# Scale and shift of x's blocks, and the gate unit's normalisation, written by ScalarE instead of VectorE in a hybrid HGRN2/gMLP block

## The chip, the cores and the metric

The kernel runs on one core of a Trainium2 chip. Its time is the device time of one execution in microseconds (us). PE is the matmul engine, PEld its weight loads, DVE the vector engine, ACT the scalar engine, POOL GpSimd, SP the engine that issues the DMAs.

## The reference

One layer of a diffusion backbone on x (2048 positions, 1024 channels) with a context of 256 positions, in fp32. Cut to what matters here:

```python
def modulate(h, shift, scale):
    return h * (1.0 + scale) + shift
...
h = modulate(rmsnorm(x, norm_mix[l]), sh1, sc1)
o, _, _ = token_mixers(h @ w_in[l], lb_f, lb_b, first, hf_c, hb_c, *mix_args)
x = x + g1 * (o @ w_out[l])
h2 = modulate(rmsnorm(x, norm_ffn[l]), sh2, sc2)
x = x + g2 * conv_ffn(h2, w_up[l], conv_w[l], conv_b[l], w_down[l], rows)
```

`token_mixers` has a gated linear recurrence (4 heads) and a gate unit (4 heads, chunks of 128 positions) on the same projection:

```python
def chunk_sgu(u, v, ln_g, ln_b, w_s, b_s):
    ...
    u = jax.nn.gelu(u, approximate=False).reshape(bsz, n, MLP_CHUNK, MLP_HEADS, MLP_DIM)
    v = jax.nn.gelu(v, approximate=False).reshape(bsz, n, MLP_CHUNK, MLP_HEADS, MLP_DIM)
    v = layernorm(v, ln_g.reshape(MLP_HEADS, MLP_DIM), ln_b.reshape(MLP_HEADS, MLP_DIM))
    z = jnp.einsum('hpq,bnqhc->bnphc', w_s.astype(v.dtype), v) + jnp.transpose(b_s)[None, None, :, :, None]
    return (u * z).reshape(bsz, t, MLP_WIDTH)
```

The change touches `modulate` of the first `h` and the inner part of `layernorm`, (v - mean) times the reciprocal deviation.

## The kernel before

**Precision.** Every large product of fp32 operands is made of three products of two halves. `split` (L131, L132) writes the high half of a tile by a cast on ACT and the low half by a subtraction on DVE or POOL; `mm3` or the loop in `run_banks` adds high x high, high x low and low x high into one PSUM bank. All matmuls are recorded at L65 and all transpositions at L69, so tile names tell them apart.

**Stages.** Until about 50 us the modulation vectors are made and the context is normalised, transposed and split (`ctx_mod`, L313). Then `run_banks` goes through a hand-written order of product banks until about 980 us: per bank eight blocks of weights (`whi`, `wlo`, split from `raw` by `split_w`, two slots that alternate) times the rows of x (`xh`, `xl`), three products for each of the eight blocks, 128x512 results in a bank with the tag `pj`, which a sink then reads. After that come the output projection and the gated MLP, up to the end.

The first banks are those of the context ("c", 256 columns wide), then "g" and "v" on x's first half, in the order `c c c c c c g c g c v c q c q c s c s s c s t c t t t`. Side work is put between the products by two queues: `Pump.slot` runs what is due, by a clock of modelled PE time (`T.t`); a generator says with `yield 1.6` how long it wants to wait. In this way:

- `x_start` and `x_first` (16 blocks of 128x512, some 55 to 95 us): rows are squared and summed on ACT (`xjk`, L231), the reciprocal deviation `rs` comes from POOL (L124, L126), DVE scales the rows `xk` (L237), PE transposes four 128x128 blocks into a bank of the tag `mi`, and `x_mod` (L239 to L244) scales and shifts the bank with the columns `a1` and `s1` into the tile `xfl` and splits it into `xh` and `xl`. For odd blocks DVE writes `xl`, for even blocks POOL.
- `x_second` (32 blocks of 128x256, some 112 to 200 us) does the same for x's second half, through `sp` into DRAM (`xh_d`, `xl_d`), from which it is loaded again later.
- the sinks: `silu` (a sigmoid `sig` on ACT and a product on DVE), `sink_gate` and `sink_gate_x` (sigmoids on ACT: `cf`, `cS`, later F and K), and `sgu` for the gate unit.

`xfl` and `sig` share one tag with two buffers. The tag `mi` has three banks, `pj` three, `sc` two.

**The gate unit.** `sv` evicts a bank with a Gelu on ACT. 4.6 us of modelled time later `ln` transposes it into an `mi` bank, takes mean and variance on DVE (`bn_stats`, `bn_aggr` into `mv`), the reciprocal deviation on POOL (`rstd`, L124 and L126), and writes `nt` in four pieces of 128x128 (L699). 7.0 us later `mix` multiplies `nt` by the position matrix (`wsT`). There are 16 such normalisations, from 141 to 976 us.

**Order.** Outside `manual_schedule` and apart from pinned instructions, a scheduler orders each engine's instructions by priorities and its own cost model. A changed engine or price thus also changes the order of neighbouring instructions.

Of the kernel before, what the change touches and what calls it, by code (L numbers as in the profile page):

```python
# [9 lines left out]
F32 = mybir.dt.float32  # L10
# [3 lines left out]
AF = mybir.ActivationFunctionType  # L14
ALU = mybir.AluOpType
# [3 lines left out]
P = 128  # L19
# [29 lines left out]
def view(t, off, dims):  # L49

    return bass.AP(t.tensor, t.offset + off, [list(t.ap[0])] + [list(d) for d in dims])
# [32 lines left out]
def tile_trunk(ctx, tc, x, c, cx, c_ctx, w_ada, b_ada, norm_mix, norm_ffn, w_in, hg_norm, sgu_g, sgu_b,  # L84
               w_sp, b_sp, w_out, w_up, conv_w, conv_b, w_down, norm_final, masks, out):
    nc = tc.nc
    V, S, G, T = nc.vector, nc.scalar, nc.gpsimd, Tensor(nc.tensor)
# [19 lines left out]
    a1 = cst.tile([P, 2, 8], F32, name="a1")  # L107
    s1 = cst.tile([P, 2, 8], F32, name="s1")
# [12 lines left out]
    def rstd(pool, ss, n, scale, bias=EPS, keep=lambda i: i, out=None):  # L121

        r = pool.tile([P, 8], F32, tag="rs", name="rs")
        keep(G.tensor_scalar(out=r[:, :n], in0=ss, scalar1=scale, scalar2=bias, op0=ALU.mult, op1=ALU.add))  # L124
        r2 = pool.tile([P, 8], F32, tag="rs2", name="rs2") if out is None else out
        G.tensor_tensor(out=r2[:, :n], in0=r[:, :n], in1=mhalf[:, :n], op=ALU.pow)  # L126
        return r2

    def split(hi, lo, raw, eng=None, keep=lambda i: i):

        keep(S.copy(hi, raw))  # L131
        (eng or G).tensor_sub(lo, raw, hi.bitcast(F32))  # L132
# [56 lines left out]
    with es1:  # L189
        ps = es1.enter_context(tc.tile_pool(name="ps1", bufs=1, space=PSUM, reuse_waits="tile"))  # L190
        p1 = es1.enter_context(tc.tile_pool(name="p1", bufs=1, reuse_waits="tile"))
        pm = es1.enter_context(tc.tile_pool(name="pm", bufs=1, reuse_waits="tile"))
# [10 lines left out]
        def bank(tag):  # L203
            return ps.tile([P, 512], F32, tag=tag, name=tag, bufs={"pj": 3, "sc": 2, "mi": 3}[tag])
# [34 lines left out]
        def x_mod(pt, which, k, hi, lo, n, eng):  # L239

            fl = pm.tile([P, 512], F32, tag="sig", name="xfl", bufs=2)
            V.tensor_scalar(out=fl[:, :n], in0=pt, scalar1=a1[:, which, k:k + 1], scalar2=s1[:, which, k:k + 1],
                            op0=ALU.mult, op1=ALU.add)
            split(hi, lo, fl[:, :n], eng)  # L244

        def rows_of(src, t0, n):
# [146 lines left out]
        def x_first(g0, xs):  # L393
            for k in range(NK):
                pt = bank("mi")
                for i in range(4):
                    pin(T.transpose(pt[:, i * P:(i + 1) * P], xs[i][:, k * P:(k + 1) * P], ident))
                sl = slice(g0 * P, g0 * P + 512)
                x_mod(pt, 0, k, xh[:, k, sl], xl[:, k, sl], 512, V if k % 2 else G)
                if k % 2:  # L400
                    yield 1.6
# [24 lines left out]
        def x_second():  # L426

            xk = pk.tile([P, 2, D], F32, tag="K", name="xk2", bufs=2, align_bytes=AL)
            sp = pk.tile([P, 4, 512], F32R, tag="K", name="sp", bufs=2, align_bytes=AL)
            xs = [xk[:, 0, :], xk[:, 1, :]]  # L430
            n = 0
            for g in range(0, NCH, 2):
                for i in range(2):
                    ld(xs[i], x_rows[NCH + g + i])
                yield 6.0
                ss = x_sums()
                x_square(xs, ss)
                x_scale(xs, ss)
                yield 6.0
                for k in range(0, NK, 2):  # L440
                    pt = bank("mi")
                    for kk in range(2):
                        for i in range(2):
                            o = kk * 256 + i * P
                            pin(T.transpose(pt[:, o:o + P], xk[:, i, (k + kk) * P:(k + kk + 1) * P], ident))
                    b = 2 * (n % 2)
                    n += 1
                    for kk in range(2):
                        sl = slice(kk * 256, kk * 256 + 256)
                        x_mod(pt[:, sl], 0, k + kk, sp[:, b, sl], sp[:, b + 1, sl], 256, V if kk else G)  # L450
                    for t, d in ((0, xh_d), (1, xl_d)):
                        st(d[:, k:k + 2, g * P:g * P + 256], sp[:, b + t, :].bitcast(F32).rearrange("p (k c) -> p k c", k=2))
                    yield 2.2
# [214 lines left out]
        def sgu(hh, h):  # L668

            z, u = {}, {}  # L670

            def both(n0):
                if n0 in z and n0 in u:
                    zt = z.pop(n0)
                    G.tensor_mul(zt, zt, u.pop(n0))
                    st(oT_d[hh][:, 4 + h, n0:n0 + 512], zt)

            def su(n0, n, pj):
                u[n0] = pm.tile([P, 512], F32, tag="gu", name="gu", bufs=2)
                S.activation(u[n0], pj, AF.Gelu)  # L680
                both(n0)

            def sv(n0, n, pj):
                gv = pm.tile([P, 512], F32, tag="vv", name="gv", bufs=2)
                S.activation(gv, pj, AF.Gelu)

                def ln():
                    pt = bank("mi")
                    for i in range(4):
                        T.transpose(pt[:, i * P:(i + 1) * P], gv[:, i * P:(i + 1) * P], ident)  # L690
                    bs = pm.tile([P, 4, 6], F32, tag="bs", name="bs", bufs=2)
                    mv = pm.tile([P, 4, 2], F32, tag="mv", name="mv", bufs=2)
                    for i in range(4):
                        V.bn_stats(out=bs[:, i, :], in_=pt[:, i * P:(i + 1) * P])
                        V.bn_aggr(out=mv[:, i, :], in_=bs[:, i, :])
                    r = rstd(pm, mv[:, :, 1], 4, 1.0)
                    nt = pm.tile([P, 512], F32, tag="nt", name="nt", bufs=2)
                    for i in range(4):
                        V.tensor_scalar(out=nt[:, i * P:(i + 1) * P], in0=pt[:, i * P:(i + 1) * P],  # L699
                                        scalar1=mv[:, i, 0:1], scalar2=r[:, i:i + 1], op0=ALU.subtract, op1=ALU.mult)  # L700

                    def mix():
                        pz = bank("mi")
                        for i in range(4):
                            T.matmul(pz[:, i * P:(i + 1) * P], nt[:, i * P:(i + 1) * P], wsT[:, h, :],
                                     start=True, stop=True)
                        V.scalar_tensor_tensor(out=nt.rearrange("p (c q) -> p c q", q=P),
                                               in0=pz.rearrange("p (c q) -> p c q", q=P), scalar=sgg[:, h:h + 1],
                                               in1=view(rh, h * P, [[0, 4], [1, P]]), op0=ALU.mult, op1=ALU.add)
                        z[n0] = nt  # L710
                        both(n0)
                    hg_q.later(mix, 7.0)
                hg_q.later(ln, 4.6)
            return su, sv

# [397 lines left out]
        i = len(seq) - 4  # L1113
# [452 lines left out]
    V = Kept(nc.vector, pin)  # L1566
# [243 lines left out]
```

## Time and profile before

| | |
|---|---|
| median of the runs | 2451.37 us (2449.67, 2451.37, 2454.72) |
| profiled execution | 2449.13 us, span 2447.3 us |
| mean granted PE clock | 0.998 |
| PE busy | 2408.3 us, 98% |
| DVE busy | 1785.5 us, 73% |
| ACT busy | 943.7 us, 39% |
| POOL busy | 873.4 us, 36% |
| DMA | 163 GB/s mean |

One execution was profiled. A row of a group gives line, engine, operation, written tile and read tiles, shapes, count, then busy time, mean ns of one, and the idle time of the engine just before, with what ended most of it. A row in the order of time gives start and duration in us, and in brackets the wait before it. "PEclk" is the granted clock of the matmul engine as a share of full speed.

### The profile page before, as it was taken

The numbers are of one execution on the slowest core, as the hardware profiler recorded it, in microseconds if no ns is written. First come the engines' busy times: TensorE is split into PE (matmuls) and PEld (weight loads), VectorE is DVE, ScalarE is ACT, GpSimd is POOL, SyncE is SP. The second block draws the span as 40 slices with busy tenths as digits, with TensorE's granted clock in tenths as the row PEclk, the third lists the DMA queues.
The fourth block names the chain that finished last, engine by engine and source line by source line (L and its number), as shares of the span: only waits on it lengthen the run. The fifth ranks groups of instructions, "written<-read, shape, count | busy, mean of one in ns | idle before, by whom it ended". The sixth has DMA issues, their size and how long they took to land.

```text
span 2447.3 us, 32836 instructions
## 1 busy us (share of the span) xinstructions
PE 2408.3 (98%) x11859; PEld 2000.8 (82%) x11859; DVE 1785.5 (73%) x2445; ACT 943.7 (39%) x1614; POOL 873.4 (36%) x795
## 2 busy tenths in 40 slices
PE   7999999999999999999999999999999999999998
PEld 4788888888888888788788888878888888888887
DVE  5867685756776776466698877769999992776875
ACT  4554334333344433354443333333333342332343
POOL 1232010110111122001688778787778870000002
PEclk9999999999999999999999999999999999999999
DMA  8365446564254234668822222562222238934645
GB/s 310 109 210 171 141 136 209 193 225 147 96 185 155 87 104 149 233 216 261 297 86 88 82 96 83 177 237 85 86 93 94 83 102 349 318 125 146 228 151 197
DMA packets 307855, 400.13 MB, mean 163 GB/s; under 512 B 33113, under 2 KB 216161, under 8 KB 304621
## 3 DMA queue, kind: packets, MB, share of 16 engines
q1 hardware_dynamic: 304404, 397.28, 48.1%
q8 instruction: 94, 1.54, 0.3%
q10 hardware_dynamic: 3289, 0.76, 0.1%
q14 instruction: 68, 0.56, 0.1%
HBM read 288.85 MB, written 109.13 MB: 163 GB/s over the span
## 4 chain that ended last, share of the span: by engine, by line
PE 40%; DVE 7%; issue 3%; POOL 2%; ACT 1%; DMA 0%; SPq 0%; POOLq 0%; ACTq 0%; DVEq 0%
PE up L65 25%; PE dn L65 15%; DVE dn L1377 3%; DVE edges L1382 1%; DVE gp L1458 1%; ACT dn L1374 1%; POOL Al L132 0%; POOL ra L1669 0%; POOL rr L1670 0%; DVE keep L1452 0%; POOL raw L1195 0%; DVE keep L1468 0%; ACT cv L1396 0%; ACT Ah L131 0%; POOL cv L1469 0%
## 5 line engine op out<-in xcount | busy, mean ns | idle before, releaser
L1377 DVE SCALAR_TENSOR_TENSOR dn<-gp,taps,dn 128x1024 f32<-128x1024 f32 x352 | 448.3, 1280 | 21.4 <-ACT dn L1374 18.1
L65 PE MATMUL up<-yf,Ah 128*128 128x512 f32 x1232 | 393.7, 389 | 0.0
L65 PE MATMUL dn<-thl,mhl 128*128 128x512 f32 x1680 | 381.5, 389 | 1.2 <-ACT thl L131 1.2
L132 POOL TENSOR_TENSOR Al<-raw,Ah 128x512 fp32r<-128x512 f32 x264 | 342.9, 1307 | 92.0 <-ACT Ah L131 79.0
L65 PEld LDWEIGHTS dn<-thl,mhl 128*128 128x128 f32 x1680 | 315.0, 188 | 67.7 <-ACT thl L131 2.0
L65 PE MATMUL pj<-xh,whi 128*128 128x512 f32 x896 | 363.1, 406 | 0.0
L65 PE MATMUL pj<-xh,wlo 128*128 128x512 f32 x896 | 350.6, 392 | 2.0 <-DVE wlo L132 2.0
L65 PE MATMUL pj<-xl,whi 128*128 128x512 f32 x896 | 351.4, 392 | 1.1 <-POOL xl L132 1.0
L65 PE MATMUL up<-xah,Al 128*128 128x512 f32 x704 | 275.6, 392 | 3.8 <-POOL Al L132 3.8
L65 PE MATMUL up<-xah,Ah 128*128 128x512 f32 x704 | 274.5, 390 | 0.6 <-ACT Ah L131 0.6
L65 PEld LDWEIGHTS up<-yf,Ah 128*128 128x128 f32 x1232 | 231.2, 188 | 48.1
L131 ACT CAST Ah<-raw 128x512 fp32r<-128x512 f32 x264 | 160.5, 618 | 278.4 <-PE up L65 208.4
L65 PE MATMUL up<-xal,Ah 128*128 128x512 f32 x528 | 205.5, 389 | 0.0
L65 PE MATMUL up<-yf,Al 128*128 128x512 f32 x528 | 205.2, 389 | 0.0
L65 PEld LDWEIGHTS pj<-xh,wlo 128*128 128x128 f32 x896 | 168.3, 188 | 38.2 <-DVE wlo L132 2.7
L65 PEld LDWEIGHTS pj<-xh,whi 128*128 128x128 f32 x896 | 168.6, 188 | 33.3 <-issue 3.5
L65 PEld LDWEIGHTS pj<-xl,whi 128*128 128x128 f32 x896 | 168.8, 188 | 32.2 <-POOL xl L132 1.9
L65 PE MATMUL dn<-wo,o 128*128 128x512 f32 x768 | 182.9, 394 | 2.1 <-ACT o L131 1.6
L580 POOL TENSOR_TENSOR K<-K,tot 128x512 f32<-128x512 f32 x40 | 50.0, 1251 | 343.9 <-PE sc L65 194.5
L65 PEld LDWEIGHTS dn<-wo,o 128*128 128x128 f32 x768 | 141.9, 188 | 31.8 <-ACT o L131 2.0
L65 PEld LDWEIGHTS up<-xah,Al 128*128 128x128 f32 x704 | 132.1, 188 | 36.5 <-POOL Al L132 9.4
L65 PEld LDWEIGHTS up<-xah,Ah 128*128 128x128 f32 x704 | 132.2, 188 | 28.0 <-ACT Ah L131 1.0
(315 smaller groups left out, 3923.7 us busy)
## 6 DMA issues: line engine op xcount, KB each, us to landing
raw<-in_w_up_dram SPq DMA_DIRECT2D x88, 512.0 KB, 4.7
mr<-m SPq DMA_DIRECT2D x85, 512.0 KB, 5.0
raw<-in_w_in_dram SPq DMA_DIRECT2D x68, 512.0 KB, 4.2
sT<-wd SPq DMA_DIRECT2D x88, 256.0 KB, 4.1
raw<-in_w_ada_dram SPq DMA_DIRECT2D x32, 512.0 KB, 3.8
yf<-yd SPq DMA_DIRECT2D x14, 1024.0 KB
m<-cv SPq DMA_DIRECT2D x22, 544.0 KB, 2.7
raw<-in_w_down_dram SPq DMA_DIRECT2D x22, 512.0 KB, 4.3
```

The source lines that it names most:

```text
L65: return self.engine.matmul(out, lhsT, rhs, **kw)
L131: keep(S.copy(hi, raw))
L132: (eng or G).tensor_sub(lo, raw, hi.bitcast(F32))
L580: e.tensor_mul(view(K2, row * W + o, src), view(K, o, src), view(tot, t0, [[4, n], [ts, 2], [0, B]]))
L1374: S.activation(cr, gt[:, 0:RH, 0:GW], AF.Identity, bias=cvb[:, f:f + 1], scale=taps[:, f:f + 1])
L1377: V.scalar_tensor_tensor(out=cr, in0=gt[:, t // 3:t // 3 + RH, t % 3:t % 3 + GW], scalar=taps[:, t * NF + f:t * NF + f + 1], in1=cr, op0=A ...
L1382: V.scalar_tensor_tensor(out=e[:, 0, :], in0=gt[:, 1, t % 3:t % 3 + GW], scalar=taps[:, t * NF + f:t * NF + f + 1], in1=e[:, 0, :], op0=AL ...
L1458: V.tensor_add(g_rows(hh, f + c, n2), quad(p, kind), quad(add, kind))
```

## The change

`x_mod`: the multiplication and addition of a block by two columns is one ACT instruction (Identity with a scale and a bias column) and not one DVE instruction. In the gate unit a tile `nm` of 128x4, minus the mean times the reciprocal deviation, is new on DVE; `nt` is then x times the reciprocal deviation plus `nm`, in four ACT instructions in place of four on DVE.

```diff
         def x_mod(pt, which, k, hi, lo, n, eng):
 
             fl = pm.tile([P, 512], F32, tag="sig", name="xfl", bufs=2)
-            V.tensor_scalar(out=fl[:, :n], in0=pt, scalar1=a1[:, which, k:k + 1], scalar2=s1[:, which, k:k + 1],
-                            op0=ALU.mult, op1=ALU.add)
+            S.activation(fl[:, :n], pt, AF.Identity, bias=s1[:, which, k:k + 1], scale=a1[:, which, k:k + 1])
             split(hi, lo, fl[:, :n], eng)
...
                     r = rstd(pm, mv[:, :, 1], 4, 1.0)
                     nt = pm.tile([P, 512], F32, tag="nt", name="nt", bufs=2)
+                    nm = pm.tile([P, 4], F32, tag="nm", name="nm", bufs=2)
+                    V.scalar_tensor_tensor(out=nm, in0=mv[:, :, 0], scalar=-1.0, in1=r[:, :4], op0=ALU.mult, op1=ALU.mult)
                     for i in range(4):
-                        V.tensor_scalar(out=nt[:, i * P:(i + 1) * P], in0=pt[:, i * P:(i + 1) * P],
-                                        scalar1=mv[:, i, 0:1], scalar2=r[:, i:i + 1], op0=ALU.subtract, op1=ALU.mult)
+                        S.activation(nt[:, i * P:(i + 1) * P], pt[:, i * P:(i + 1) * P], AF.Identity,
+                                     bias=nm[:, i:i + 1], scale=r[:, i:i + 1])
```

## The prediction

> **What bounds the kernel now.** I read the page's busy times first, then the busy times by stretch, then who PE waits for, then the order in time of PE, ACT, DVE and POOL in the one stretch where PE has holes.
>
> ```profile
> span 2447.3 us, 32836 instructions
> PE 2408.3 (98%) x11859; PEld 2000.8 (82%) x11859; DVE 1785.5 (73%) x2445; ACT 943.7 (39%) x1614; POOL 873.4 (36%) x795
> ```
>
> ```profile
> core 0: us, PE busy (x) PEld busy (x) DVE busy (x) ACT busy (x) POOL busy (x), PEclk, DMA share, GB/s
> 50.00:100.00 50.00, 45.12 (x282) 37.84 (x282) 44.69 (x77) 26.49 (x50) 15.21 (x12) 0.97 0.35 109
> 100.00:150.00 50.00, 49.61 (x289) 42.85 (x289) 30.84 (x73) 27.16 (x49) 10.83 (x15) 1.00 0.56 175
> 150.00:200.00 50.00, 49.73 (x273) 42.29 (x272) 37.12 (x84) 24.83 (x45) 21.64 (x23) 1.00 0.62 201
> 200.00:1020.00 820.00, 811.09 (x4599) 697.46 (x4599) 544.25 (x857) 305.99 (x594) 113.04 (x118) 1.00 0.47 158
> 1020.00:2447.00 1427.00, 1413.98 (x6265) 1163.20 (x6263) 1104.52 (x1312) 539.47 (x844) 709.97 (x618) 1.00 0.47 161
> ```
>
> PE, the matmul engine, is busy in 2408.3 of 2447.3 us: it is the bound, and only the 39 us in which it stands idle, or new idle time, can move the end. The stretches say where it stands. The edited lines run from just before the first cast of `xfl` (the row of 56.19 below) to the last `nt`, which starts at 974.8 us by the line's own view:
>
> ```profile
> L699 DVE TENSOR_SCALAR nt<-mi,mv,rs x64: 398/402/410, 141.2 to 974.8; 128x128 f32<-128x128 f32 x64
> ```
>
> In 50 to 100 us PE loses 50.00 - 45.12 = 4.88 us while DVE is busy for 44.69 of 50; from 100 to 200 us it loses 0.66 us, from 200 to 1020 us 8.9 us in 820. So the stretch that matters is 50 to 100 us, where the first half of x is scaled, shifted and split. There the clock granted is 0.97, elsewhere 1.00, so no term below comes from the clock.
>
> **What is removed and added.** These groups carry the prices (busy time, mean ns of one, idle time before them):
>
> ```profile
> L242 DVE TENSOR_SCALAR xfl<-mi,a,s 128x256 f32<-128x256 f32 x32 | 16.1, 532 | 5.3 <-POOL sp L132 3.2 <-PE mi L69 2.0
> L242 DVE TENSOR_SCALAR xfl<-mi,a,s 128x512 f32<-128x512 f32 x16 | 12.7, 802 | 2.5 <-POOL xl L132 2.0 <-PE mi L69 0.4
> L699 DVE TENSOR_SCALAR nt<-mi,mv,rs 128x128 f32<-128x128 f32 x64 | 21.9, 403 | 18.5 <-POOL rs L126 18.5
> ```
>
> ```profile
> L313 ACT ACTIVATE xfl<-mi,s,a 128x256 f32<-128x256 f32 x4 | 2.2, 562 | 5.1 <-DVE s L300 3.9 <-DVE cl L318 1.3
> L549 ACT ACTIVATE cS<-pj 128x256 f32<-128x256 f32 x4 | 1.5, 382 | 0.0
> L977 ACT ACTIVATE sig<-pj 128x512 f32<-128x512 f32 x32 | 19.1, 596 | 38.6 <-PE pj L65 38.1 <-POOL xl L132 0.4
> L622 ACT COPY cdh<-mi 128x128 f32<-128x128 f32 x8 | 2.1, 264 | 7.4 <-DVE hf L623 4.7 <-PE mi L65 2.8
> ```
>
> DVE loses 48 scale-and-shifts and 64 normalisations: 16.1 + 12.7 + 21.9 = 50.7 us. It gains 16 `nm` of 128x4; the nearest row is the 128x4 operation below, 0.16 us, so 2.6 us in all.
>
> ```profile
> 50.27 0.16 DVE L300 TENSOR_TENSOR s<-sc,bc 128x4 f32<-128x4 f32 x1 [0.37 <-PE sc L65]
> ```
>
> ACT gains 112 instructions. The trace has the very form in L313: 128x256 out of PSUM with scale and bias from a column per partition, 562 ns, against 382 ns for L549, the same size without them: 180 ns for the two columns. Added to 596 ns (L977, 128x512) that is 0.78 us, added to 264 ns (L622, 128x128) 0.44 us. ACT gains 16 x 0.78 + 32 x 0.56 + 64 x 0.44 = 59 us. On an engine that is busy for 39% that costs nothing by itself; what counts is the order, because ACT now does both halves of a chain that DVE and ACT shared.
>
> For the same instruction a column operand's price also stands in the Trainium skill, "ScalarE: Activation LUTs", section "What ACT_TABLE_LOAD costs": 186 ns plus 0.833 ns per element plus about 93 ns per column. An estimate by it is 0.80 us for 128x512 and 585 ns for 128x256; L313 measured 562, so it is a little dear here, and the sum below would be 0.1 us longer by it.
>
> **50 to 100 us, step by step.** The rows of PE, ACT, DVE and POOL in the order of time (start, duration, in brackets the wait before):
>
> ```profile
> 64.18 0.39 PE L65 MATMUL pj<-ch,wlo 128*128 128x256 f32 x1 [1.01 <-DVE wlo L132]
> 67.70 0.48 PE L65 MATMUL pj<-xh,whi 128*128 128x512 f32 x1
> 69.43 0.50 PE L65 MATMUL pj<-xh,wlo 128*128 128x512 f32 x1 [0.90 <-DVE wlo L132]
> 75.54 0.30 PE L69 MATMUL mi<-ident,xk 128*128 128x128 f32 x1
> 81.53 0.66 PE L69 MATMUL mi<-ident,xk 128*128 128x128 f32 x4 [0.29 <-DVE xfl L242]
> 82.39 0.66 PE L69 MATMUL mi<-ident,xk 128*128 128x128 f32 x4 [0.20 <-DVE hb L623]
> 87.42 0.66 PE L69 MATMUL mi<-ident,xk 128*128 128x128 f32 x4
> 89.44 0.50 PE L65 MATMUL pj<-xl,whi 128*128 128x512 f32 x1 [0.62 <-POOL xl L132]
> 93.07 0.50 PE L65 MATMUL pj<-xl,whi 128*128 128x512 f32 x1 [0.37 <-POOL xl L132]
> ```
>
> ```profile
> 56.19 1.14 ACT L131 CAST xh<-xfl 128x512 fp32r<-128x512 f32 x2
> 59.46 0.38 ACT L549 ACTIVATE cf<-pj 128x256 f32<-128x256 f32 x1
> 62.33 1.05 ACT L231 ACTIVATE xjk<-xk 128x1024 bf16<-128x1024 f32 x1
> 63.38 0.36 ACT L549 ACTIVATE cf<-pj 128x256 f32<-128x256 f32 x1
> 64.95 1.04 ACT L131 CAST whi<-raw 128x1024 fp32r<-128x1024 f32 x1
> 83.52 0.60 ACT L977 ACTIVATE sig<-pj 128x512 f32<-128x512 f32 x1 [0.44 <-POOL xl L132]
> ```
>
> ```profile
> 67.33 2.05 DVE L132 TENSOR_TENSOR wlo<-raw,whi 128x1024 fp32r<-128x1024 f32 x1
> 74.64 2.74 DVE L237 TENSOR_SCALAR xk<-xk,rs 128x1024 f32<-128x1024 f32 x4
> ```
>
> ```profile
> 67.01 1.29 POOL L132 TENSOR_TENSOR xl<-xfl,xh 128x512 fp32r<-128x512 f32 x1 [4.42 <-ACT xh L131]
> 73.08 0.34 POOL L124 TENSOR_SCALAR rs<-xss 128x4 f32<-128x4 f32 x1
> 73.50 1.11 POOL L126 TENSOR_TENSOR rs<-rs,mhalf 128x4 f32<-128x4 f32 x1
> ```
>
> *What goes.* PE's waits for DVE (1.01 at 64.18, 0.90 at 69.43, 0.29 at 81.53, 0.20 at 82.39) and for POOL's `xl` (0.62 and 0.37) are late products of DVE's queue and of the chain behind `xfl`: 3.39 us. I count all as gone and put in their place what the changed order makes.
>
> *A weight's cast behind two pairs.* In the changed program's order ACT does per pair of blocks `xfl, xfl, xh, xh`, and the cast `whi` of 64.95 stands two pairs later, behind the second pair and one more `xjk`. Two neighbours on ACT overlap by 0.10 us (56.19: two 0.62 casts in 1.14), so from the `cf` at 59.46, which PE releases: two `cf` 0.56, pair 1.36 + 1.04, `xjk` 1.05 (62.33 to 63.38), `cf` 0.27, `xjk` 1.05, `cf` 0.27, pair 2.40, `xjk` 1.05 = 9.05, so `whi` runs 68.5 to 69.6 instead of 64.95 to 66.0. PE wants it for the product of 67.70, which it now reaches 1.01 earlier, at 66.7: a new wait of 2.9 us. The low half `wlo` (2.05 at 67.33, beside POOL's subtraction of 67.01; without that I take 1.2) is ready at 70.8, two products later PE waits 0.75 more.
>
> *The rows of the second group.* ACT then does `xjk` 1.05, a copy 0.27 and the pair's 1.36 before `xh` of block 6 ends at 72.8. POOL's order is fixed: `xl` of block 6 (1.29) stands ahead of the `rs` pair (73.08 to 74.6), so `rs` is done at 75.6 where it was done at 74.6, and DVE's scaling (74.64 before) begins 1.0 later. PE comes to the first transposition (75.54 row) at 75.1 and gets its operand at 76.4: about 1.2 us of waiting.
>
> *The last block's bank.* Three PSUM banks hold the transposed blocks; block 7 of the second group needs block 4's bank back. Before, it stood behind some sixteen products (82.39 to 87.42), in the new order behind one. Block 4's `xfl` stands on ACT behind `sig`, which shares its two buffers with `xfl` and waits for POOL's `xl` (0.44 at 83.52 already). Laid out from block 0's transposes at 78.5: two pairs with POOL's 1.29 between them, `xl` of block 2 done at 85.5, `sig` 0.5, two copies 0.54, `xfl` 0.78: 87.4. PE is there at 85.4: 2.0 us. Towards the end `xh` and `xl` of block 6 come 0.3 late each: 0.6.
>
> New waits 2.9 + 0.75 + 1.2 + 2.0 + 0.6 = 7.45; less 3.39 is +4.1. Hand-overs between engines, which I left out of these chains, I estimate at 0.4 together. **+4.5 us**, bounds: -1 where the casts fit into ACT's gaps after all, +7 where all waits of DVE's stay too.
>
> **100 to 200 us.** The second half of x goes in 16 pairs of 128x256: ACT gets 32 x 0.56 and 16 x 0.44 = 25 us on top of 52 of 100. PE now waits there for a bank once:
>
> ```profile
> 146.96 0.66 PE L69 MATMUL mi<-ident,xk 128*128 128x128 f32 x4 [0.39 <-DVE xfl L242]
> ```
>
> The same bank is now released by an ACT that first does four `nt` and a `whi`; and in the last group the fourth set of transpositions stands behind one product where it stood behind four, so PE asks for its bank three products (1.4 us by the row of 67.70) earlier. I take 0.4 for the first and 0.6, under half of the 1.4, for the second: **+1.0 us** (0 to +2.5).
>
> **The gate unit.** `nt` moves with its wait: DVE's 18.5 us of idle time before `nt` waits for POOL's `rs`; now `nm` waits there on DVE, and ACT's `nt` waits behind `nm`. Behind a waiting `nt` stand casts of weights and evictions of products; the bank it reads is asked for only some 20 products later, and the matmul on `nt` is put 7 us later. From 200 to 1020 us ACT is busy in 306 of 820: I take 0 (-1 to +8, see the second rival).
>
> **Sum.** The profiled execution took 2449.13 us, 1.8 over its span. +4.5 + 1.0 + 0 = +5.5: 2454.6. The median of the runs, 2451.37, is 2.24 above the profiled one: **2456.9 us**.
>
> **Rivals.** *DVE's relief is what counts* (faster). DVE is at 89% in 50 to 100 us, PE's waits there are mostly for it, and later it also waits for DVE:
>
> ```profile
> PE sc L65 <- DVE Q L503: 2.0, 2, 1.3
> PE mi L69 <- DVE on L727: 1.4, 2, 1.0
> ```
>
> If ACT's queue makes no new waits, 3.39 + 0.39 go, and of these 3.4 us at most the first 2.0: -5.8, 2445.6 us. Against it: in the later chains `nt` isn't near, and POOL's `rk` is what `on` waits for. It decides if `whi` is cast before 66.7. Chance 0.15.
>
> *ACT blocked behind the mean* (slower still). Each of 16 normalisations holds ACT for 18.5/16 = 1.2 us of waiting and 4 x 0.44 = 1.8 of work. If in eight of them a `whi` or an eviction behind it is late by 1 us, +8 on the forecast: 2464.9 us. It decides where an eviction behind `nt` comes later than PE's next demand for its bank. For: PE loses 8.9 us in 200 to 1020 us already, so not every chain there has slack. Against: ACT is idle for 514 of those 820 us. Chance 0.20.
>
> *Nothing moves*: ACT's gaps take the work, old waits and new ones cancel, 2451.4 us, chance 0.10.
>
> *ACT is far dearer per element.* Three times DVE's 802 ns makes 38.5 us for the sixteen 128x512 beside 26.5 of ACT's own in 50 us: 65 in 50, some 15 us longer, 2466.4. Against it stand 562 ns on ACT (L313) and 532 on DVE (L242), same size, same PSUM source. Chance 0.02.
>
> By the Trainium skill, "ScalarE: Activation LUTs", section "Rules for kernel authors", plain multiplying and adding belong on VectorE, up to about three times faster per element in bf16; for f32 out of PSUM the trace disagrees, and no bf16 case is here.
>
> **How the numbers follow.** About 0.2% (4.9 us) is what a measurement of this kernel can tell from no change. The forecast has 0.53, two thirds of it (0.36) over +4.9. Slower 0.36 + 0.20 + 0.02 = 0.58; within 0.17 + 0.10 = 0.27; faster 0.15. Its own range is 2452.5 to 2460; 2449 to 2466 takes in most of the second rival and leaves out the first.
>
> **What would show it.** Right: PE's busy time in 50 to 100 us below 43 us, a wait of PE for ACT's `whi` of 2 to 3 us near 67, one for ACT's `xfl` of about 2 near 86, DVE below 34 us there; `xfl` at 0.78 and 0.56, `nt` at 0.44 us. Wrong: PE's waits for `wlo` gone with none for ACT in their place; or a PE that loses several us between 200 and 980 us.

## The result, and the profile after

The changed kernel takes 2467.32 us (median of six executions, 2464.59 to 2469.46), the kernel before, run beside it, 2454.22 us (six, 2449.67 to 2456.18): ratio 1.0061, 95% interval 1.0050 to 1.0072, or 13.1 us slower. The forecast was 5.5 us slower, and 2466 the upper end of its range. Some of the distance is the kernel before itself: 2451.37 us in the three executions that the forecast started from, 2.9 less than in the six.

The page's head and the busy times by stretch of the changed kernel (columns as in the prediction, up to 1020 us):

```profile
span 2464.9 us, 32883 instructions
PE 2412.5 (98%) x11859; PEld 2004.6 (81%) x11859; DVE 1751.7 (71%) x2349; ACT 988.7 (40%) x1726; POOL 867.3 (35%) x795
```

```profile
50.00:100.00 50.00, 42.97 (x253) 36.55 (x253) 35.96 (x57) 35.32 (x63) 14.97 (x11) 0.90 0.35 108
100.00:150.00 50.00, 49.70 (x288) 42.87 (x286) 21.75 (x47) 32.33 (x62) 7.68 (x12) 1.00 0.45 147
150.00:200.00 50.00, 43.53 (x239) 36.89 (x240) 26.82 (x63) 31.00 (x64) 15.07 (x20) 0.98 0.56 182
200.00:1020.00 820.00, 807.61 (x4585) 695.28 (x4584) 528.87 (x812) 322.17 (x644) 117.16 (x120) 1.00 0.47 157
```

PE is busy for 42.97 us in 50 to 100 us (45.12 before), and the page of before had nothing like the third row: 43.53 in 150 to 200 us, where it was 49.73. DVE is relieved, though by less than the prediction named (35.96 us for 44.69 in 50 to 100 us, where it said below 34), and it brings nothing that shows. The clock is down too, 0.90 and 0.98 in the two bad stretches.

One and the same eviction on ACT, compared in both profiles, shows where the time goes: the eviction of `vv` at 99.8 us comes 3.8 us later, the third one of `F` at 209.4 us 11.7, and the last of the gate unit at 977.7 us 15.4. So some 4 us come before 100 us, 8 between 100 and 209, and 4 after that, of which part is chance (see the second profile of before below). The third eviction of `F`, before and after:

```profile
209.41 0.59 ACT L556 ACTIVATE F<-pj 128x512 f32<-128x512 f32 x1
221.14 0.59 ACT L555 ACTIVATE F<-pj 128x512 f32<-128x512 f32 x1
```

The prices of the instructions themselves were right: 0.78, 0.56 and 0.44 us were forecast.

```profile
L242 ACT ACTIVATE xfl<-mi,s,a 128x512 f32<-128x512 f32 x16 | 11.7, 783 | 8.2 <-PE mi L69 7.0 <-POOL xl L132 0.7 <-DVE xl L132 0.4
L242 ACT ACTIVATE xfl<-mi,s,a 128x256 f32<-128x256 f32 x32 | 16.7, 565 | 12.0 <-PE mi L69 6.0 <-POOL sp L132 5.4 <-DVE sp L132 0.5
L700 ACT ACTIVATE nt<-mi,nm,rs 128x128 f32<-128x128 f32 x64 | 24.1, 457 | 52.1 <-DVE nm L698 52.1
```

783, 565 and 457 ns. What wasn't forecast is the last figure of the `nt` row: ACT stood idle for 52.1 us waiting for `nm`, where DVE, in the same place, had stood for 18.5.

**Where PE stands in 50 to 200 us.** The waits over 2 us in PE's order of time:

```profile
69.06 0.80 PE L65 MATMUL pj<-xh,whi 128*128 128x512 f32 x1 [3.02 <-ACT whi L131]
87.81 0.66 PE L69 MATMUL mi<-ident,xk 128*128 128x128 f32 x4 [2.03 <-ACT xfl L242]
```

```profile
168.51 0.33 PE L69 MATMUL mi<-ident,xk 128*128 128x128 f32 x1 [2.20 <-DVE xk L237]
198.42 0.45 PE L69 MATMUL mi<-ident,xk 128*128 128x128 f32 x1 [3.68 <-DVE xk L237]
```

The first two are those that the prediction laid out (2.9 near 67 and 2.0 near 86 us). The other two it had no term for. How they come about is read from the order of time of the other engines. First the kernel before: ACT evicts `gu`, DVE's `nt` is beside it, and SP issues the loads of the next two rows of x, one before and one after the store of the gate unit's product.

```profile
149.77 0.59 ACT L680 ACTIVATE gu<-pj 128x512 f32<-128x512 f32 x1
182.63 1.05 ACT L231 ACTIVATE xjk<-xk 128x1024 bf16<-128x1024 f32 x1
```

```profile
148.50 0.42 SPq L434 DMA_DIRECT2D xk<-in_x_dram  x1
152.88 0.33 SPq L676 DMA_DIRECT2D oT<-nt  x1
153.79 0.45 SPq L434 DMA_DIRECT2D xk<-in_x_dram  x1
```

Now the changed kernel, ACT, POOL, SP and DVE:

```profile
152.88 0.70 ACT L131 CAST sp<-xfl 128x256 fp32r<-128x256 f32 x2
155.17 1.51 ACT L700 ACTIVATE nt<-mi,nm,rs 128x128 f32<-128x128 f32 x4 [1.59 <-DVE nm L698]
156.70 0.63 ACT L679 ACTIVATE gu<-pj 128x512 f32<-128x512 f32 x1
163.06 1.06 ACT L231 ACTIVATE xjk<-xk 128x1024 bf16<-128x1024 f32 x1 [2.62 <-DMA xk<-in_x_dram]
```

```profile
157.41 1.29 POOL L674 TENSOR_TENSOR nt<-nt,gu 128x512 f32<-128x512 f32 x1 [2.29 <-ACT gu L679]
```

```profile
158.72 0.33 SPq L675 DMA_DIRECT2D oT<-nt  x1
159.15 0.87 SPq L433 DMA_DIRECT2D xk<-in_x_dram  x2
```

```profile
167.70 1.42 DVE L237 TENSOR_SCALAR xk<-xk,rs 128x1024 f32<-128x1024 f32 x2 [2.89 <-POOL rs L126]
```

ACT has done the casts at 153.6 us and stands in `nt` for 1.59 us, though the bank of `gu` had its last product by 152.3; `gu` runs at 156.70, where 149.77 + 3.8 = 153.6 was to be had. POOL's product waits for `gu`, its store on SP waits for POOL, and behind the store stand both loads of x's rows (159.15, where the second one went out at 153.79). The rows land at 163.06, then come `xjk`, `rs`, and DVE's scaling at 167.70, and PE has waited 2.20 us. Of the instructions in that chain the change moved only `nt` and its `nm`. The order on SP is new too: before, the first load went out ahead of the store, now both stand behind it.

The second wait has the same head, and is shorter to tell:

```profile
190.89 1.24 DVE L698 SCALAR_TENSOR_TENSOR nm<-mv,rs 128x4 f32<-128x4 f32 x1 [1.48 <-POOL rs L126]
197.52 1.42 DVE L237 TENSOR_SCALAR xk<-xk,rs 128x1024 f32<-128x1024 f32 x2 [5.38 <-POOL rs L126]
```

```profile
189.09 0.60 ACT L679 ACTIVATE gu<-pj 128x512 f32<-128x512 f32 x1 [2.74 <-PE pj L65]
192.17 1.50 ACT L700 ACTIVATE nt<-mi,nm,rs 128x128 f32<-128x128 f32 x4 [2.48 <-DVE nm L698]
193.55 1.06 ACT L231 ACTIVATE xjk<-xk 128x1024 bf16<-128x1024 f32 x1
```

`xjk` stands on ACT behind `nt`, which waited 2.48 us for `nm`; before, it ran right behind `gu` (182.63). Its sums go to POOL, from there to DVE's scaling at 197.52, and PE waits 3.68 us. `xjk` runs 3.9 us after the end of `gu`; 2.48 of that is `nt`'s wait, and most of the rest its own work (1.50).

**The clock.** PE alone, in stretches of 3 us (PE busy, granted clock, DMA share, GB/s):

```profile
69.00:72.00 3.00, 2.90 (x6) 0.50 0.13 36
72.00:75.00 3.00, 3.00 (x11) 0.50 0.47 139
75.00:78.00 3.00, 3.00 (x14) 0.94 0.00 0
90.00:93.00 3.00, 3.00 (x10) 0.59 0.75 289
198.00:201.00 3.00, 2.58 (x10) 0.54 0.00 0
```

After the wait of 3.02 us the clock granted is 0.50 for 6 us, after that of 2.03 us and after the last it is lower too. After the one of 2.20 us it stays at 1.00. Products of 128x512 start 0.43 us apart at 0.50 and 0.23 us apart at 1.00.

### The profile page after: what moved, and what is told of

Read it like the earlier page. It is cut to its first block, busy times and chain, and to the rows that moved or that the text cites. A ratio compares the mean times of both kernels' runs of the same rounds, so it can differ in the third digit from the quotient of the medians.

```text
span 2464.9 us, 32883 instructions
## 1 busy us (share of the span) xinstructions
PE 2412.5 (98%) x11859; PEld 2004.6 (81%) x11859; DVE 1751.7 (71%) x2349; ACT 988.7 (40%) x1726; POOL 867.3 (35%) x795
## 4 chain that ended last, share of the span: by engine, by line
PE 34%; DVE 9%; issue 4%; POOL 3%; ACT 2%; DMA 1%; SPq 0%; POOLq 0%; ACTq 0%; DVEq 0%
PE up L65 20%; PE dn L65 14%; DVE dn L1378 4%; DVE edges L1383 2%; POOL Al L132 1%; DVE gp L1459 1%; ACT dn L1375 1%; DMA raw<-in_w_up_dram 0%; POOL ra L1670 0%; DVE keep L1469 0%; POOL cv L1470 0%; DVE keep L1453 0%; POOL rr L1671 0%; POOL raw L1196 0%; ACT cv L1397 0%
```

## The experiments

Theory A: three separate costs, one in each of the stretches above, by ACT's order (`whi` and `xfl` behind the pairs; `nt` standing behind the mean). Theory B: the 48 scale-and-shifts on ACT are the cost, and `nt` is harmless. "Mark" is the shift of the eviction of `F` at 209.4 us against the first profile of before, "mark of `vv`" that of the one at 99.8 us. A mark comes from one execution: the six kernels that put x's whole first half on ACT and change nothing else there have marks of `vv` from +3.8 to +5.4, so a microsecond or two between two marks says little.

### One part alone: `x_mod` on ACT, `nt` on DVE

```diff
-            V.tensor_scalar(out=fl[:, :n], in0=pt, scalar1=a1[...], scalar2=s1[...], op0=ALU.mult, op1=ALU.add)
+            S.activation(fl[:, :n], pt, AF.Identity, bias=s1[...], scale=a1[...])
```

> The scale and shift of x's blocks on ACT, the gate unit's normalisation left on DVE. Theory A (three separate costs: 4.1 us from ACT's queue in 50 to 100 us, 7.9 us in 100 to 200 us from ACT standing in nt behind the mean and holding the row loads of x's second half, 3.4 us later from the same stand): the waits for whi near 67 us (3.0) and for xfl near 86 us (2.0) are there, the waits for xk near 166 and 195 us (2.5 and 3.7) are gone, nothing changes after 200 us; about 4 to 6 us slower than before. Theory B (the 48 scale-and-shifts on ACT are the whole cost, nt is harmless): the waits for xk are there too, 11 to 15 us slower.

Measured: 2458.83 beside 2454.71 us, ratio 1.0017 (1.0008 to 1.0025), 4.1 us slower; mark +4.2. The waits for `whi` (3.02) and `xfl` (2.04) are there, those for `xk` are not. Theory A's numbers; theory B's 11 to 15 us are out.

### The other part alone: `nt` on ACT, `x_mod` on DVE

The edit is the second hunk of the change, without the first.

> The normalisation on ACT, the scale and shift of x's blocks left on DVE. Theory A: the stretch of 50 to 100 us as before (PE idle 4.6 us), PE waits for xk near 165 and 190 us together 3 to 6 us with a lower clock behind them, two waits of 1 us for nt before the transpositions of K near 480 and 665 us; 8 to 11 us slower. Theory B: no wait over 0.5 us that before doesn't have; within 2 us of before.

Measured: 2459.79 beside 2454.71 us, ratio 1.0020 (1.0011 to 1.0029), 5.1 us slower; mark +6.1. PE's rows and clock:

```profile
191.69 0.45 PE L69 MATMUL mi<-ident,xk 128*128 128x128 f32 x1 [3.22 <-DVE xk L237]
```

```profile
189.00:192.00 3.00, 0.31 (x2) 0.75 0.00 1
192.00:195.00 3.00, 3.00 (x15) 0.50 0.15 18
195.00:198.00 3.00, 3.00 (x13) 0.61 0.90 327
```

```profile
PE mi L69 <- ACT nt L701: 2.0, 2, 1.0
```

Up to 100 us nothing moves (mark of `vv` +0.2). Then PE waits once for `xk`, 3.22 us, and the clock falls to 0.50. The two waits of 1.0 us before K's transpositions are there as well: a bank that `nt` still reads is asked for. The mark is more than the wait: 3 us at 0.50 and 3 us at 0.61 lose an estimated 2.7 us of full speed, and 3.2 + 2.7 is the 5.9 us between the two marks. The time is below the 8 to 11 us expected; of the two waits for `xk` only the later one comes with this part alone. The parts' sum, 9.2 us, is 4 short of the whole by the medians, and 1.4 by the marks (10.3 of 11.7). Neither part alone has the wait near 166 us. That it needs both, `nt` that waits and an ACT whose queue is filled with `xfl`, is my reading; the order on SP differs too, since in this run both loads go out ahead of the store (147.54 and 149.90 us).

### Only x's first half on ACT, and only the second half

```diff
+            if n == 512:        # the other run: n == 256
+                S.activation(fl[:, :n], pt, AF.Identity, bias=s1[...], scale=a1[...])
+            else:
                 V.tensor_scalar(...)
```

> Only the 16 blocks of 128x512 of x's first half are scaled and shifted on ACT. Theory A: 3.8 to 4.3 us later than before at 100 us (3.0 for whi and 2.0 for xfl, less the old waits, the rest from a granted clock of about 0.9 in 50 to 100 us), and no more is added after that: about 4 us slower. Theory B: the same here, so this run tells only whether the cost of 50 to 100 us is free of the second half.

> Only the 32 blocks of 128x256 of x's second half are scaled and shifted on ACT. Theory A: ACT has room there (25 us more beside 52 of 100) and nothing stands waiting on it, so PE's idle time in 100 to 200 us stays under 1.5 us: within 1.5 us of before. Theory B: PE waits for xk near 165 and 190 us, 5 to 8 us slower.

Measured: the first half 2457.93 beside 2454.71 us, ratio 1.0015 (1.0006 to 1.0024), 3.2 us slower; the second half 2454.50, ratio 1.0000 (0.9991 to 1.0010). The second half's blocks cost nothing on ACT by themselves; the cost of `x_mod` is that of 50 to 100 us.

### The clock in the wait for `whi`

```diff
                 if i == 3:
                     x_scale(xs, ss2)
+                    idle = bank("sc")
+                    for j in range(12):
+                        pin(T.engine.matmul(idle[:, :P], ones, ident, start=True, stop=True))
```

> Only x's first half scaled and shifted on ACT, and twelve matmuls of 128x128 on constants, which nothing reads, put into the time in which PE waits for whi near 68 us. Theory E (the wait itself costs 3.0 us, and the half clock granted after it as much again): the clock granted stays at 1.00 from 69 to 78 us, the products there start 0.23 us apart and not 0.43, and the mark at 80 us comes 2 to 3 us earlier than without the fill, though PE still can't go on before whi. Theory F (the slow products after the wait have another cause, such as the weights' low half or DVE): the products stay 0.43 apart and the mark doesn't move.

Measured, on the kernel with only the first half on ACT: 2454.95 beside 2454.46 us, ratio 1.0004 (0.9995 to 1.0013). PE in stretches of 3 us, and its next wait:

```profile
69.00:72.00 3.00, 2.65 (x20) 1.00 0.00 0
72.00:75.00 3.00, 2.49 (x14) 1.00 0.43 124
```

```profile
78.38 0.30 PE L69 MATMUL mi<-ident,xk 128*128 128x128 f32 x1 [1.69 <-DVE xk L237]
```

The clock stays at 1.00, so theory E is right on its cause: it is the pause that lowers it. Its price was wrong: the mark of `vv` is +5.3 with the fill and +5.4 without. A faster PE only comes earlier to the rows of the second group, `xk`, and waits 1.69 us for them (0.56 without the fill); the transposition starts at 78.38 us, and at 78.50 without the fill. These rows come from ACT's chain of squares, and their time is set there; the slow clock was hidden by that wait. The medians differ by 2.7 us against their own kernels before, with intervals that overlap, so that the fill gains anything isn't shown.

### `xfl` apart from `sig`

```diff
-            fl = pm.tile([P, 512], F32, tag="sig", name="xfl", bufs=2)
+            fl = pm.tile([P, 512], F32, tag="ot" if n == 512 else "sig", name="xfl", bufs=2)
```

> Only x's first half scaled and shifted on ACT, and xfl of these blocks in two buffers that it doesn't share with sig. If the wait of 2.0 us for xfl near 86 us comes from the buffers that sig shares with xfl, it falls to 1 us or less and the clock granted stays at 1.00 after it: 1.5 to 3 us less than with the shared buffers at 100 us. If it comes from ACT's order alone (xfl behind sig, two cS copies and a pair of casts), it stays over 1.7 us.

Measured, with only the first half on ACT: 2459.04 beside 2454.46 us, ratio 1.0018 (1.0009 to 1.0027), no better than with the shared buffers.

```profile
87.31 0.66 PE L69 MATMUL mi<-ident,xk 128*128 128x128 f32 x4 [0.99 <-ACT xfl L243]
92.13 0.50 PE L65 MATMUL pj<-xl,whi 128*128 128x512 f32 x1 [0.73 <-DVE xl L132]
94.87 0.50 PE L65 MATMUL pj<-xl,whi 128*128 128x512 f32 x1 [0.63 <-POOL xl L132]
```

The wait for `xfl` falls from 2.03 to 0.99 us, as expected of the shared buffers, so half of the term was the buffers. Two waits for `xl` (0.73 and 0.63) stand behind it, where the run with the shared buffers had one of 0.39. The mark of `vv` is +4.3 for +5.4, less than the 1.5 to 3 us expected and within the spread of the marks; whether the chain behind ACT gives the gain back stays open.

### `nt` issued later

```diff
-                    for i in range(4):
-                        S.activation(nt[...], pt[...], AF.Identity, bias=nm[:, i:i + 1], scale=r[:, i:i + 1])
+                    def norm():
+                        for i in range(4):
+                            S.activation(nt[...], pt[...], AF.Identity, bias=nm[:, i:i + 1], scale=r[:, i:i + 1])
+                    hg_q.later(norm, 4.0)
```

> The whole change, but the four ACT instructions of nt are put in 4.0 us of modelled PE time after nm, so that they need not wait for the mean; ACT then does gu before the second nt. Theory A (ACT's stand behind nm holds gu and the stores on SP, and with them the row loads of x's second half): the wait for xk near 166 us (2.5) is gone, that near 195 us (3.7) falls to under 2, the waits for nt before K's transpositions (2 x 1.0) are gone or move; 50 to 100 us unchanged. About 6 us slower than before in place of 13. Theory C (ACT's extra work, not the standing, makes the second half late): both waits for xk stay within 0.5 us and the time stays 12 to 14 us over before.

Measured: 2467.09 beside 2454.46 us, ratio 1.0054 (1.0041 to 1.0066), 12.6 us slower: the expectation of 6 was missed. The wait near 166 us is gone (0.30 is left), but that near 195 us is 3.22. The mark is +9.2 where it was +11.7, a gain that the time doesn't show. ACT's order there shows why:

```profile
189.57 1.51 ACT L701 ACTIVATE nt<-mi,nm,rs 128x128 f32<-128x128 f32 x4 [2.01 <-DVE nm L698]
190.96 1.06 ACT L231 ACTIVATE xjk<-xk 128x1024 bf16<-128x1024 f32 x1
```

The scheduler, which orders by priority, still put `nt` ahead of `xjk`, so this edit took the standing away in one of the two places alone. It neither proves nor refutes theory A for the second place; the run with the first four on DVE does.

### The store out of SP's way

```diff
-                    st(oT_d[hh][:, 4 + h, n0:n0 + 512], zt)
+                    G.dma_start(oT_d[hh][:, 4 + h, n0:n0 + 512], zt)
```

> The whole change, but the store of the gate unit's product goes to POOL's own DMA queue and no longer stands on SP ahead of the row loads of x's second half. Theory A: the load that was issued at 159.2 us goes out at about 155 us, when the last store of sp is through, and the wait for xk near 166 us (2.5) is gone or under 0.5; the one near 195 us stays, since there the stores of sp and xjk itself stand behind nt on ACT. 9 to 11 us slower than before. Theory D (the load was late for another reason, its buffer or the transpositions): the wait near 166 us stays at 2 us or more, 13 us slower.

Measured: the loads go out at 156.79 us in place of 159.15, and the wait near 166 us falls to 0.51 in two parts. So the store on SP was the link. The mark hardly moves, though (+11.5 for +11.7), and the time is 2471.47 beside 2454.46 us, ratio 1.0074 (1.0061 to 1.0086): 17.0 us slower, where 9 to 11 were expected. Five waits for loads of `xl` and one of 1.12 for `whi` come later, in 510 to 546 us.

```profile
PE pj L65 <- DMA xl<-xl_d: 3.3, 5, 0.8
PE pj L65 <- ACT whi L131: 4.9, 3, 3.0
```

Whether POOL's queue or the moved DMAs cause these stays open.

### The first four normalisations on DVE

```diff
+                    late = "x1" in done
...                  # nm is made only where late is true
                     for i in range(4):
+                        if late:
                             S.activation(nt[...], ...)
+                        else:
+                            V.tensor_scalar(out=nt[...], ..., op0=ALU.subtract, op1=ALU.mult)
```

> The whole change, but the first four of the 16 normalisations, those that run while x's second half is scaled, stay on DVE; the other twelve and all of x's blocks are on ACT. Theory A (the four early ones hold ACT ahead of gu, xjk and the casts of sp, and with them the row loads): the waits for xk near 166 (2.5) and 195 us (3.7) both fall under 0.5, the granted clock stays at 1.00 there, and what is left is the 4 us of 50 to 100 us and two waits of 1 us for nt before K's transpositions: 5 to 6 us slower than before. Theory G (all 16 cost about the same, some 0.5 us each): 10 us slower.

Measured: 2460.75 beside 2453.07 us, ratio 1.0032 (1.0019 to 1.0044), 7.7 us slower, against 13.1 for the whole change; mark +5.0 where it was +11.7.

```profile
150.00:200.00 50.00, 49.57 (x282) 42.27 (x281) 34.98 (x80) 31.30 (x63) 17.34 (x23) 1.00 0.65 206
214.43 0.59 ACT L555 ACTIVATE F<-pj 128x512 f32<-128x512 f32 x1
```

PE is busy for 49.57 us of the 50 again, at a clock of 1.00, and the only wait for `xk` left there is 0.27 us, as in the kernel before. Four of the 16 normalisations make 6.7 us at the mark, and 5.4 us by the medians, whose intervals don't overlap. The time itself lies between theory A's 5 to 6 and theory G's 10, and its interval, 4.7 to 10.8 us, holds both; the mark decides, since by theory G four of the 16 make only 2 us. The run takes `nt`'s wait and its work off ACT together, so which of the two delays the rest is not shown. What the other twelve cost stays open: against `x_mod` alone it is 3.6 us by the medians, with intervals that overlap, and 0.3 us by the last eviction of the gate unit (+7.1 and +6.8).

### Odd blocks alone, and without both costly places

```diff
+            if n == 512 and k % 2:      # the other run: n == 256 or k % 2, and the first four nt on DVE
+                S.activation(...)
+            else:
                 V.tensor_scalar(...)
```

> Only the eight odd blocks of x's first half are scaled and shifted on ACT, the even ones on DVE. The cast whi then stands one block further forward on ACT: by theory A the wait for whi near 68 us falls from 3.0 to under 1, the one for xfl near 86 us is gone or under 0.5, the waits for DVE's wlo (1.0 and 0.9) shrink too: within 2 us of before, rather below it. By theory B (each block on ACT costs some 0.25 us) 2 us slower.

> The change without both places that cost: in x's first half only the odd blocks on ACT, in the second half all, and the first four normalisations on DVE, the other twelve on ACT. Theory A: no wait of PE over 1.1 us between 55 and 400 us, clock at 1.00 from 60 us; 0 to 3 us slower than before, the rest being nt before K's transpositions. If DVE's relief is worth anything later, it shows here as a median below that of before.

Measured: the odd blocks alone 2456.72 beside 2453.07 us, ratio 1.0015 (1.0006 to 1.0023), 3.6 us slower, mark +3.8; with the second half and the twelve late `nt` on ACT too 2456.81, ratio 1.0018 (1.0009 to 1.0027), 3.7 us slower, mark +2.1. With odd blocks the wait for `whi` is 1.38 us in the one run and 0.37 in the other, and a new one of 1.1 for `vv` stands behind it. The first was expected to be no slower than 2 us, the second 0 to 3, and both were slower; by the medians halving the number on ACT does not halve the cost. By the marks of `vv` it is less plain: +3.7 in the first run, whose clock falls to 0.50 in 72 to 74 us, and +1.9 in the second, whose clock stays at 1.00. No version with any of x's first half on ACT came out below the kernel before.

### The kernel before, once more

> The kernel before, unchanged, profiled once more, since one profiled execution is what all marks so far are taken against. Marks up to 200 us should come within 1 us of the first profile; if the short waits for DVE and for DMAs between 400 and 550 us, which also grew in runs whose median didn't move, are chance, they differ here by 1 to 3 us too.

Measured: 2454.08 us. Its mark is +1.2, its last eviction of the gate unit +3.7, so the first profile was a short one, by some 2.5 us after 209 us:

```profile
462.82 1.35 PE L65 MATMUL sc<-Q,K 128*128 128x128 f32 x10 [1.65 <-DVE Q L503]
480.04 1.16 PE L65 MATMUL mi<-wsT,nt 128*128 128x128 f32 x8 [1.48 <-ACT fs L836]
```

The first of these waits was 1.35 us in the first profile, the second 0.34. Waits in 400 to 550 us differ by a microsecond from one execution to the next, and of the 3.7 us that the changed kernel loses after 209 us 1.2 are left against this profile. The run with the second half alone, whose time did not move, even has +6.5 at the last eviction of the gate unit. What the change costs after 209 us can't be told from single profiles; what the trace of the changed kernel shows there is two waits of 1.0 before K's transpositions.

## Why the prediction was wrong

**50 to 100 us: right in sum and in place, by luck in part.** +4.5 was forecast; the mark of `vv` shows +3.8, `x_mod` alone costs 4.1 us and its first half 3.2. The wait for `whi` (2.9 forecast, 3.02), the last block's bank (2.0, 2.03) and the end of DVE's and POOL's waits came as laid out. The 0.75 for `wlo` and the 1.2 for the second group's rows did not show in the changed kernel, whose PE ran at half clock into both. With the clock held up by the fill, both waits are there, at 0.53 and 1.69. So the chain was right; that "no term below comes from the clock" was wrong, and harmless here only since another wait was next. Behind the wait near 195 us nothing hid it: the row of 198 to 201 us (2.58 us busy at 0.54) alone loses an estimated 1.2 us.

**100 to 200 us: the step that failed.** +1.0 was forecast (0 to 2.5), and 7.9 came (3.8 to 11.7). I looked for late banks there, and none came late: `x_mod`'s 32 blocks cost nothing (ratio 1.0000). The work of the gate unit's first four normalisations, which fall into this stretch, was in the sum (16 x 0.44). What I left out is what stands behind `nt` on ACT in it while `nt` waits and works: `gu`, and with it a store and the row loads on SP; the casts `sp`, and with them stores on SP; `xjk`, and with it `rs` and `xk`. I listed casts and evictions behind a waiting `nt` and asked only when banks were wanted again. With the four left on DVE, 6.7 us of the mark went. Most of it hangs on `xjk`: with `nt` alone on ACT that one wait and the slow clock behind it make 5.9 us, while without the wait near 166 us the mark was 0.2 (store moved) to 2.5 us (`nt` issued later) earlier. My signs of being wrong named a PE that loses time after 200 us, and none for this stretch.

**The gate unit: 0 was taken, and the price of a wait was mis-sized.** I gave each `nt` 1.2 us of waiting, from DVE's idle time. On DVE the statistics themselves stood ahead of it, so most of the wait for them was work. On ACT nothing of that chain stands ahead, and the wait measured 52.1/15 = 3.5 us. That size is not what failed, though: the first four, those that cost, waited 0.25 to 2.48 us, on average 1.4, and the long waits come later. Late in the kernel ACT has room for it, as forecast, except for two waits of 1.0 us for a bank; that the bank "is asked for only some 20 products later" failed there.

**The rivals.** "ACT blocked behind the mean" (0.20, +8 on the forecast, 2464.9 us) had the mechanism and nearly the size, in the wrong place: I priced it as `whi` and evictions late in eight of the 16, and it was x's rows, late in two of the first four. "DVE's relief" found no support: the twelve late normalisations and 32 blocks off DVE gained nothing that showed. "Nothing moves" is out, by an interval of 1.0050 to 1.0072. ACT was not dear per element: 783 ns against 802 on DVE.

## What to carry to other kernels

Before moving a waiting instruction to another engine, list everything that stands behind it there, and follow each one to the queue that it feeds, DMA issue included; four normalisations, each with 0.25 to 2.48 us of waiting and 1.5 of work on an engine that is busy for 40% of the kernel, cost 5 to 7 us, mostly through a square that stood behind one of them. Price the wait by when the new engine gets to it, and not by the old engine's idle time, which counts only what its own work didn't cover. When a long pause of PE is part of a sum, look at what comes next before adding the slow clock after it: the next wait may have been there anyway, or there may be none, and the slow clock counts in full.

## What the runs showed of the hardware that I hadn't expected

**The clock after a pause.** In 55 to 215 us eleven pauses of 3.0 to 3.7 us, in eight runs, were followed by a granted clock of 0.50 to 0.68 in the 3 us behind them. Of eight pauses of 2.0 to 2.2 us two lowered it: 2.03 us did in the changed kernel (0.59 in 90 to 93 us), and the same 2.03 us did not in the run with the first half alone (row below). With the odd blocks two waits of 1.38 and 1.10 us, with two products between them, were enough (0.50 in 72 to 74 us). By the Trainium skill, "TensorE: Matmul & The Clock Gate", section "Part 1: The HAM clock gate (the "warmup" mystery)", the clock halves after an idle window of about 3.4 us in a window that runs free. Pauses of 3.02 and 2.03 us are shorter than that and lowered it, so here the measurement decides; a window whose position matters would fit the two outcomes of 2.03 us, but no run here shows where it lies.

```profile
90.00:93.00 3.00, 3.00 (x17) 1.00 0.59 157
```

**`nm` beside POOL.** Thirteen of the sixteen instructions of 128x4 took 0.15 to 0.17 us. The other three, at 154.45, 190.89 and 910.25 us, took 0.69, 1.24 and 1.25:

```profile
L698 DVE SCALAR_TENSOR_TENSOR nm<-mv,rs x16: 155/164/1245, 145.5 to 988.7; 128x4 f32<-128x4 f32 x16
```

```profile
190.83 1.29 POOL L674 TENSOR_TENSOR nt<-nt,gu 128x512 f32<-128x512 f32 x1
```

The one at 190.89 began 0.06 us behind POOL's product of 190.83, both reading two operands out of SBUF, and ended with it; ACT's `nt` waited for it. The other two ended with a POOL instruction of two operands in the same way, that of 154.45 with the subtraction of 154.38 (0.74 us), and beside the thirteen POOL ran nothing. The first `nm` of the changed kernel took 0.16 us with POOL idle; in the run with `nt` alone the same one ran beside POOL's subtraction and took 0.69. By the Trainium skill, "GPSIMD Engine Reference", section "1. Specifications", POOL shares its SBUF interfaces with VectorE, with contention where a VectorE instruction has two SBUF inputs; these rows agree.
